# A decoder trunk on one core: the second layer's memory softmax turned by VectorE squares and transfers instead of TensorE transposes

## The chip, the core and the metric

The kernel runs on one core of a Trainium2 chip. A core has TensorE (PE, matrix products and transposes), VectorE (DVE), ScalarE (ACT), GpSimd (POOL) and SyncE (SP), which here issues DMA transfers. Each engine executes its own queue in order; engines wait for one another by semaphores. The metric is device microseconds of one execution.

## The reference

The reference is a trunk of two layers over 256 positions of width 2048, in float32. Layer A mixes with a gated spatial unit, layer B with latent attention (12 heads); beside either stands a cross-attention of 4 heads into 256 memory tokens, and after each a gated feed-forward part. The change concerns the memory heads of layer B, which stand beside the latent attention:

```python
def mla_attention(q_lat, g_q_lat, w_uq, w_uk, w_uv, c_kv, k_rope, cos, sin):
...
        qa = jnp.einsum('bqhn,rhn->bqhr', qn, w_uk)
        s = (jnp.einsum('bqhr,bkr->bhqk', qa, c_kv)
             + jnp.einsum('bqhp,bkp->bhqk', qr, k_rope)).astype(jnp.float32) * scale
        q_pos = i * Q_BLOCK + jnp.arange(Q_BLOCK)
        s = jnp.where(k_pos[None, :] <= q_pos[:, None], s, -jnp.inf)
        p = jax.nn.softmax(s, axis=-1).astype(c_kv.dtype)
        o_lat = jnp.einsum('bhqk,bkr->bqhr', p, c_kv)
        return jnp.einsum('bqhr,rhv->bqhv', o_lat, w_uv)
...

def memory_attention(q_m, mem, g_mem, w_mem_kv):
    B, S, _ = q_m.shape
    M = mem.shape[1]
    q = q_m.reshape(B, S, MEM_HEADS, MEM_HEAD_DIM)
    kv = rmsnorm(mem, g_mem) @ w_mem_kv
    k = kv[..., :MEM_W].reshape(B, M, MEM_HEADS, MEM_HEAD_DIM)
    v = kv[..., MEM_W:].reshape(B, M, MEM_HEADS, MEM_HEAD_DIM)
    s = jnp.einsum('bshd,bmhd->bhsm', q, k).astype(jnp.float32) * (MEM_HEAD_DIM ** -0.5)
    p = jax.nn.softmax(s, axis=-1).astype(v.dtype)
    return jnp.einsum('bhsm,bmhd->bshd', p, v).reshape(B, S, MEM_W)

...
        mo = memory_attention(q_m, mem, g_mem[l], w_mem_kv[l])
        x = x + jnp.concatenate([main, mo], axis=-1) @ w_out[l]
```

The memory's keys and values depend on no layer's activations and are made at the start.

## The kernel before

**Weights.** Nearly all the work is matrix products with weights that are streamed once from HBM. `chunk()` loads a piece of 512 KB (384 KB for `w_uq`) by a DMA on SP into a tile `raw`. ACT copies it, rounded, to `whi` (L124), and DVE makes the rest `wlo` = `raw` - `whi` (L125). There are four buffers each of `raw`, `whi` and `wlo`, so loads run a few pieces ahead of PE. PE multiplies both halves with activations that are split the same way (`mm_fm`, L161, L162 and L164; `gemm_tm`, L192 to L194). Right behind each load's issue `chunk()` calls `self.pending.some()`, which issues the transfers that were asked for behind that load, if any.

**The order.** The code is written stage by stage, and a scheduler lays each engine's instructions into one static order at compile time; the order of the code is a priority, not the final order. Where the code says `manual_schedule` for SP, SP's instructions stay in the order of the code.

**Layer B's loop.** The 12 latent heads go in six pairs. For pair i `queries(i)` loads two pieces of `w_uq` and makes the pair's queries; their rotary part is made by DVE (a shuffle L795, L797 to L799) and split by ACT and DVE (L868, L869). `keys(i)` loads a piece of `w_uk`. `scores(h)` makes a head's scores in PSUM (L887, L889); DVE adds the mask and takes the maximum (L894), ACT the exponential with its sum (L899), and DVE scales by the reciprocal of the sum (L902, L904). `turn(h)` transposes the probabilities in three blocks on PE (L911, against an identity) with a copy from PSUM by ACT (L913), and `attend(h)` multiplies with the values (L920, L921). In pair i the scores are those of pair i-1's heads, and the turns and products those of pair i-2's. `values()` loads two pieces of `w_uv`, in pairs 2 and 4.

**Memory heads of layer B.** One a pair, between that work: `memory_scores` (head i in pair i: scores L527, maximum L532, exponential L540, reciprocal L541, scaling by DVE L546), `memory_turn` in the next pair (four PE transposes of 128x128, L554, and a copy by ACT, L558), and `memory_out` one pair later (L565).

**Memory heads of layer A.** These are turned in another way. All four heads' probabilities lie in one tile `pm`, scaled by ACT (L544). DVE transposes each 32x32 block by itself with a stream transpose, 1024 columns at a time ("a square", L727), into a tile `small`; then sixteen transfers within SBUF (L731), 64 KB each in pieces of 128 bytes, set each block where the transposed matrix has it. They are issued on SP, two behind each of eight loads.

Of the kernel before, what the change touches and what calls it, by code (L numbers as in the profile page):

```python
# [8 lines left out]
F32 = mybir.dt.float32  # L9
# [62 lines left out]
class Pending(list):  # L72
# [4 lines left out]
    def ask(self, steps, counts):  # L77
        for n in counts:
            self.append(steps[:n])
            steps = steps[n:]  # L80
        assert not steps


class Kernel:
# [438 lines left out]
    def memory_scores(self, l, h, q, pool, p=None):  # L523
        nc = self.nc
        acc = self.psum()
        for sb in range(2):
            nc.tensor.matmul(  # L527
                acc[:, sb * S : (sb + 1) * S], q[:, sb * P : (sb + 1) * P], self.kT[l][:, h, :], start=True, stop=True
            )
        scale = 128 ** -0.5  # L530
        mx = self.tmp(pool, [P, 2], "mx", 4)
        nc.vector.tensor_reduce(mx, acc.rearrange("p (a m) -> p a m", a=2), AX.X, ALU.max)  # L532
        nc.vector.tensor_scalar(mx, mx, -scale, None, ALU.mult)
        by_act = p is not None
        if p is None:
            p = self.tmp(pool, [P, 2, 2, P], "mp", 2)
        a4 = acc.rearrange("p (a m c) -> p a m c", a=2, m=2)
        den = self.tmp(pool, [P, 2], "den", 4)
        for sb in range(2):
            nc.scalar.activation(p[:, sb], a4[:, sb], AF.Exp, bias=mx[:, sb : sb + 1], scale=scale, accum_out=den[:, sb : sb + 1])  # L540
        nc.vector.reciprocal(den, den)  # L541
        for sb in range(2):
            if by_act:
                nc.scalar.activation(p[:, sb], p[:, sb], AF.Copy, scale=den[:, sb : sb + 1])  # L544
            else:
                nc.vector.tensor_scalar(p[:, sb], p[:, sb], den[:, sb : sb + 1], None, ALU.mult)  # L546
        return p

    def memory_turn(self, p, pool, bufs=2):
        nc = self.nc  # L550
        acc = self.psum()
        for mb in range(2):
            for sb in range(2):
                nc.tensor.transpose(  # L554
                    acc[:, mb * S + sb * P : mb * S + (sb + 1) * P], p[:, sb, mb], self.ident
                )
        pT = self.tmp(pool, [P, 512], "pT", bufs)
        nc.scalar.activation(pT, acc, AF.Copy)  # L558
        return pT
# [102 lines left out]
    def layer_a(self):  # L662
# [4 lines left out]
        with ExitStack() as ctx:  # L667
# [50 lines left out]
            small = small.rearrange("p (b n c) -> p b n c", b=4, c=32)  # L718
            lanes = lambda i: slice(32 * i, 32 * i + 32)
# [5 lines left out]
            def squares(k):  # L725
                src = pm[:, 1024 * k : 1024 * (k + 1)].rearrange("p (n b c) -> p n b c", n=8, b=4)
                nc.vector.transpose(small[:, :, 8 * k : 8 * k + 8, :].rearrange("p b n c -> p n b c"), src)  # L727

            def place(q, b):
                out = pm[lanes(b)].rearrange("p (n q c) -> p n q c", n=16, q=4)[:, :, q, :]  # L730
                nc.sync.dma_start(out=out, in_=small[lanes(q), b])  # L731

# [4 lines left out]
            mhooks = {2: each(scores, 0, 1), 4: each(scores, 2, 3) + each(squares, 0)}, {0: each(squares, 1)}, {5: each(out, *range(MH))}  # L737
            for c in range(3):
# [11 lines left out]
                if c == 1:  # L750
                    self.pending.ask([lambda q=q, b=b: place(q, b) for q in range(4) for b in range(4)], [0] * 6 + [2] * 8)
# [5 lines left out]
    def layer_b(self):  # L757
# [9 lines left out]
        with tc.tile_pool(name="lb", bufs=1) as lb:  # L767
# [41 lines left out]
            acc = self.psum()[:, :S]  # L809
# [39 lines left out]
            qn, qr, kn, pa, pm = {}, {}, {}, {}, {}  # L849
# [73 lines left out]

            def mscores(h):
                pm[h] = self.memory_scores(1, h, qm[:, h, :], lp)

            def mturn(h):
                pm[h] = self.memory_turn(pm[h], lp, 3)

            def mout(h):  # L930
                self.memory_out(1, h, pm.pop(h), hl)

            n = GH // 2
            for i in range(n):
# [173 lines left out]
```

## Time and profile before

| what | value |
|---|---|
| median of three runs | 2045.46 us (2045.2 to 2045.59) |
| the profiled execution's own time | 2045.34 us |
| its span, first to last instruction | 2043.6 us |
| mean granted TensorE clock | 0.999 |
| busy: PE, DVE, ACT, POOL | 100%, 66%, 51%, 5% of the span |
| read from HBM | 387.88 MB, 191 GB/s over the span |
| layer B's pair loop (from the first memory head's scores to the last one's output) | 1145.39 to 1211.4 us |

A profile row names engine, source line, operation, the tile written and the tiles read, and a count. Times are microseconds from the span's start. A busy time of PE includes matmuls that wait inside its pipeline for one another, and a duration is longer than the distance between two starts, since the next instruction begins before the last has ended; so costs on a full engine are read from distances. An idle time before an instruction is given with the engine that ended it.

### The profile page before, as it was taken

To read this page: it belongs to the slowest core of one execution; us is meant where nothing else is said; L and a number is where in the kernel's file an instruction comes from. 1 tells how busy PE (TensorE), PEld (TensorE's weight loads), DVE (VectorE), ACT (ScalarE), POOL (GpSimd) and SP (SyncE) were. 2 spreads that over 40 slices of the span, in tenths; PEclk is the share of its full clock that TensorE was granted. 3 is DMA by queue.
4 is the path that set the end of the run, shared out by engine and by line. 5 is a ranking of instruction groups with operands and counts; after the bars stand their busy time and mean duration, and the time that the engine had idled before them with its cause. 6 is when DMAs were issued, how large, how long until landed. Compare 5 with 4: busy or idle time off the path is not lost.

```text
span 2043.6 us, 38986 instructions
## 1 busy us (share of the span) xinstructions
PE 2034.7 (100%) x16216; PEld 1968.7 (96%) x16216; DVE 1359.0 (66%) x1853; ACT 1042.7 (51%) x1347; POOL 94.5 (5%) x125
## 2 busy tenths in 40 slices
PE   9999999999999999999999999999999999999998
PEld 8989999999999999999999999999988999889997
DVE  6866667767656666457689875776655667656675
ACT  6754644555435454345545665455544455434553
POOL 0000013000000000000052001300000000000000
PEclk9999999999999999999999999999999999999999
DMA  8575855666666666566565544578766666566654
GB/s 309 188 228 175 196 181 186 204 190 194 197 193 190 197 195 196 191 195 194 188 196 182 174 130 155 186 206 219 225 196 195 188 200 191 194 196 188 197 185 155
DMA packets 228306, 395.67 MB, mean 194 GB/s; under 512 B 39328, under 2 KB 45856, under 8 KB 228000
## 3 DMA queue, kind: packets, MB, share of 16 engines
q1 hardware_dynamic: 227840, 392.65, 62.5%
q8 instruction: 127, 2.08, 0.4%
q14 instruction: 51, 0.42, 0.1%
q10 hardware_dynamic: 288, 0.52, 0.1%
HBM read 387.88 MB, written 2.10 MB: 191 GB/s over the span
## 4 chain that ended last, share of the span: by engine, by line
PE 99%; issue 0%; DVE 0%; ACT 0%; POOLq 0%; POOL 0%
PE ps L161 26%; PE ps L162 26%; PE ps L164 26%; PE ps L192 6%; PE ps L194 6%; PE ps L193 6%; PE ps L887 0%; PE ps L499 0%; PE ps L498 0%; PE ps L501 0%; PE ps L565 0%; PE ps L527 0%; PE ps L704 0%; PE ps L920 0%; PE ps L889 0%; PE ps L302 0%
## 5 line engine op out<-in xcount | busy, mean ns | idle before, releaser
L125 DVE TENSOR_TENSOR wlo<-raw,whi 128x1024 fp32r<-128x1024 f32 (+1 forms) x672 | 818.8, 1235 | 610.6 <-issue 408.8
L124 ACT ACTIVATE whi<-raw 128x1024 fp32r<-128x1024 f32 (+1 forms) x672 | 705.3, 1056 | 795.9 <-PE ps L162 583.7
L161 PE MATMUL ps<-xhl,whi 128*128 128x256 f32 x3264 | 752.1, 277 | 0.0
L162 PE MATMUL ps<-xhl,whi 128*128 128x256 f32 x3264 | 750.2, 276 | 0.0
L161 PEld LDWEIGHTS ps<-xhl,whi 128*128 128x128 f32 x3264 | 612.6, 188 | 0.3
L162 PEld LDWEIGHTS ps<-xhl,whi 128*128 128x128 f32 x3264 | 612.6, 188 | 0.3
L164 PE MATMUL ps<-xhl,wlo 128*128 128x256 f32 x3264 | 403.2, 276 | 0.0
L164 PEld LDWEIGHTS ps<-xhl,wlo 128*128 128x128 f32 x3264 | 385.1, 188 | 0.0
L161 PE MATMUL ps<-h,whi 128*128 128x256 f32 x704 | 161.6, 276 | 0.0
L162 PE MATMUL ps<-h,whi 128*128 128x256 f32 x704 | 161.5, 276 | 0.0
L620 DVE SCALAR_TENSOR_TENSOR c<-a,cT,c 128x255 f32<-128x255 f32 (+1 forms) x352 | 146.3, 479 | 0.0
L193 PE MATMUL ps<-wlo,h 128*128 128x512 f32 (+1 forms) x364 | 139.0, 382 | 0.0
L194 PE MATMUL ps<-whi,h 128*128 128x512 f32 (+1 forms) x364 | 138.7, 382 | 0.0
L192 PE MATMUL ps<-whi,h 128*128 128x512 f32 (+1 forms) x364 | 138.3, 382 | 0.0
L162 PEld LDWEIGHTS ps<-h,whi 128*128 128x128 f32 x704 | 131.9, 188 | 0.0
L161 PEld LDWEIGHTS ps<-h,whi 128*128 128x128 f32 x704 | 131.9, 188 | 0.0
L617 ACT ACTIVATE c<-a,cT 128x256 f32<-128x256 f32 x176 | 91.6, 591 | 77.1 <-DVE a L242 77.1
L161 PE MATMUL ps<-mainhl,whi 128*128 128x256 f32 x512 | 118.0, 277 | 0.0
L162 PE MATMUL ps<-mainhl,whi 128*128 128x256 f32 x512 | 117.9, 276 | 0.0
L162 PEld LDWEIGHTS ps<-mainhl,whi 128*128 128x128 f32 x512 | 96.1, 188 | 0.0
L161 PEld LDWEIGHTS ps<-mainhl,whi 128*128 128x128 f32 x512 | 96.1, 188 | 0.0
L164 PE MATMUL ps<-h,wlo 128*128 128x256 f32 x704 | 86.9, 276 | 0.0
(252 smaller groups left out, 1969.1 us busy)
## 6 DMA issues: line engine op xcount, KB each, us to landing
raw<-in_w_ffn_up SPq DMA_DIRECT2D x352, 512.0 KB, 4.1
raw<-in_w_ffn_down SPq DMA_DIRECT2D x176, 512.0 KB, 4.7
raw<-in_w_out SPq DMA_DIRECT2D x64, 512.0 KB, 4.4
raw<-in_w_in_a SPq DMA_DIRECT2D x56, 512.0 KB, 4.3
raw<-in_w_mem_kv SPq DMA_DIRECT2D x30, 512.0 KB, 5.4
raw<-in_w_in_b SPq DMA_DIRECT2D x16, 512.0 KB, 4.3
raw<-in_w_uq SPq DMA_DIRECT2D x12, 384.0 KB, 3.5
raw<-in_w_kv_a SPq DMA_DIRECT2D x8, 512.0 KB, 4.5
```

The costliest lines, as they stand in the source:

```text
L124: nc.scalar.activation(hi[:, :n], raw[:, :n], AF.Copy)
L125: nc.vector.tensor_tensor(lo[:, :n], raw[:, :n], hi[:, :n].bitcast(F32), ALU.subtract)
L161: mm(acc, wh, x[:, :S], start=first, stop=False)
L162: mm(acc, wh, x[:, S:], start=False, stop=False)
L164: mm(acc, wl, x[:, :S], start=False, stop=last)
L192: mm(acc, xh, wh, start=first, stop=False)
L193: mm(acc, xh, wl, start=False, stop=False)
L194: mm(acc, xl, wh, start=False, stop=last)
L617: nc.scalar.activation(c[:, i, :], a[:, i, :], AF.Identity, scale=w(2), bias=w(3))
L620: nc.vector.scalar_tensor_tensor(o, a[:, i, : S - 2 + j], w(j), o, ALU.mult, ALU.add)
```

## The change

Layer A's way of turning is made a class `Turn` (squares, transfers), and layer B uses it too. Layer A's work and its order stay as they were on every engine. In layer B:

- all four memory heads' scores are made in pair 0, into one stretch of the tile `scratch`, and scaled by ACT;
- the two squares are made in pair 1, into a new tile `small`;
- sixteen transfers within SBUF are asked for at pair 3, two behind each of the next eight loads; SP keeps the order of the code throughout the loop;
- the transposes and the copies of `memory_turn` are gone, and all four outputs are made behind the last pair.

```diff
+class Turn:
+    def __init__(self, nc, p, small, n):
+        self.nc, self.p, self.n = nc, p, n
+        self.small = small.rearrange("p (b n c) -> p b n c", b=4, c=32)
+
+    def squares(self, first, count):
+        src = self.p[:, first * P : (first + count) * P].rearrange("p (n b c) -> p n b c", n=count, b=4)
+        self.nc.vector.transpose(self.small[:, :, first : first + count, :].rearrange("p b n c -> p n b c"), src)
+
+    def place(self, q, b):
+        lanes = lambda i: slice(32 * i, 32 * i + 32)
+        out = self.p[lanes(b)].rearrange("p (n q c) -> p n q c", n=self.n, q=4)[:, :, q, :]
+        self.nc.sync.dma_start(out=out, in_=self.small[lanes(q), b])
+
+    def places(self):
+        return [lambda q=q, b=b: self.place(q, b) for q in range(4) for b in range(4)]
 
 
 class Kernel:
...
-    def memory_scores(self, l, h, q, pool, p=None):
+    def memory_scores(self, l, h, q, pool, p):
...
-        by_act = p is not None
-        if p is None:
-            p = self.tmp(pool, [P, 2, 2, P], "mp", 2)
         a4 = acc.rearrange("p (a m c) -> p a m c", a=2, m=2)
         den = self.tmp(pool, [P, 2], "den", 4)
         for sb in range(2):
             nc.scalar.activation(p[:, sb], a4[:, sb], AF.Exp, bias=mx[:, sb : sb + 1], scale=scale, accum_out=den[:, sb : sb + 1])
         nc.vector.reciprocal(den, den)
         for sb in range(2):
-            if by_act:
-                nc.scalar.activation(p[:, sb], p[:, sb], AF.Copy, scale=den[:, sb : sb + 1])
-            else:
-                nc.vector.tensor_scalar(p[:, sb], p[:, sb], den[:, sb : sb + 1], None, ALU.mult)
-        return p
-
-    def memory_turn(self, p, pool, bufs=2):
-        nc = self.nc
-        acc = self.psum()
-        for mb in range(2):
-            for sb in range(2):
-                nc.tensor.transpose(
-                    acc[:, mb * S + sb * P : mb * S + (sb + 1) * P], p[:, sb, mb], self.ident
-                )
-        pT = self.tmp(pool, [P, 512], "pT", bufs)
-        nc.scalar.activation(pT, acc, AF.Copy)
-        return pT
+            nc.scalar.activation(p[:, sb], p[:, sb], AF.Copy, scale=den[:, sb : sb + 1])
...
+            pm = scratch[:, 2 * GW : 2 * GW + MH * 512]
+            memory = Turn(nc, pm, lp.tile([P, MH * 512], F32, name="small"), 4 * MH)
+
             def mscores(h):
-                pm[h] = self.memory_scores(1, h, qm[:, h, :], lp)
-
-            def mturn(h):
-                pm[h] = self.memory_turn(pm[h], lp, 3)
+                self.memory_scores(1, h, qm[:, h, :], lp, pm[:, 512 * h : 512 * (h + 1)].rearrange("p (m a c) -> p a m c", m=2, a=2))
 
             def mout(h):
-                self.memory_out(1, h, pm.pop(h), hl)
-
-            n = GH // 2
-            for i in range(n):
-                queries(i)
-                keys(i)
-                if i >= 2:
-                    turn(2 * i - 4)
-                    turn(2 * i - 3)
-                if i in (2, 4):
-                    values(i // 2)
-                if i >= 1:
-                    scores(2 * i - 2)
-                    scores(2 * i - 1)
-                if i >= 2:
-                    attend(2 * i - 4)
-                    attend(2 * i - 3)
-                if i < MH:
-                    mscores(i)
-                if 1 <= i <= MH:
-                    mturn(i - 1)
-                if 2 <= i <= MH + 1:
-                    mout(i - 2)
+                self.memory_out(1, h, pm[:, 512 * h : 512 * (h + 1)], hl)
+
             each = lambda f, *hs: [lambda h=h: f(h) for h in hs]
-            for f in each(scores, 10, 11) + each(turn, 8, 9):
-                f()
-            hooks = {0: each(attend, 8, 9) + each(turn, 10, 11), 2: each(attend, 10, 11)}
-            self.w_out(1, hl, [12, 13, 14, 15] + list(range(12)), hooks)
+            run = lambda fs: [f() for f in fs]
+            with tc.manual_schedule(engines={mybir.EngineType.SP}):
+                for i in range(GH // 2):
+                    if i == 3:
+                        self.pending.ask(memory.places(), [2] * 8)
+                    queries(i)
+                    keys(i)
+                    if i == 0:
+                        run(each(mscores, *range(MH)))
+                    if i == 1:
+                        run([lambda k=k: memory.squares(8 * k, 8) for k in range(2)])
+                    if i >= 2:
+                        run(each(turn, 2 * i - 4, 2 * i - 3))
+                    if i in (2, 4):
+                        values(i // 2)
+                    if i >= 1:
+                        run(each(scores, 2 * i - 2, 2 * i - 1))
+                    if i >= 2:
+                        run(each(attend, 2 * i - 4, 2 * i - 3))
+                run(each(mout, *range(MH)) + each(scores, 10, 11) + each(turn, 8, 9))
+                hooks = {0: each(attend, 8, 9) + each(turn, 10, 11), 2: each(attend, 10, 11)}
+                self.w_out(1, hl, [12, 13, 14, 15] + list(range(12)), hooks)
             ctx.close()
 
     def run(self):
```

The first place is SP's queue around the fourth pair's loads of `w_uq` (`raw` is the tile that a load fills; the line numbers of the changed program differ). Before, from the last piece of `w_uv`:

```order
L114 DMA raw_13827<-in_w_uv 128x2x512
L114 DMA raw_13920<-in_w_uq 128x2x384
L114 DMA raw_13944<-in_w_uq 128x2x384
L114 DMA raw_13983<-in_w_uk 128x4x256
L114 DMA raw_14099<-in_w_uq 128x2x384
```

Changed; the transfers are the rows with `scratch<-small`:

```order
L132 DMA raw_13847<-in_w_uv 128x2x512
L132 DMA raw_13915<-in_w_uq 128x2x384
L96 DMA scratch<-small 32x16x32 x2
L132 DMA raw_13941<-in_w_uq 128x2x384
L96 DMA scratch<-small 32x16x32 x2
L132 DMA raw_13982<-in_w_uk 128x4x256
L96 DMA scratch<-small 32x16x32 x2
L132 DMA raw_14075<-in_w_uq 128x2x384
```

The pair's second load of `w_uq` now stands behind the first two transfers, and each of the following loads behind two more. The transfers read what both squares have written.

The second place is DVE in pair 0, from the first memory head's maximum; before, one maximum stood there between two `wlo` and the other heads' came a pair apart. Changed:

```order
L550 TENSOR_REDUCE mx_13540<-ps_13537 128x2
L550 TENSOR_REDUCE mx_13552<-ps_13549 128x2
L551 TENSOR_SCALAR mx_13540<-mx_13540 128x2
L550 TENSOR_REDUCE mx_13564<-ps_13561 128x2
L551 TENSOR_SCALAR mx_13552<-mx_13552 128x2
L551 TENSOR_SCALAR mx_13564<-mx_13564 128x2
L556 RECIPROCAL den_13543<-den_13543 128x2
L556 RECIPROCAL den_13555<-den_13555 128x2
L143 TENSOR_TENSOR wlo_13613<-raw_13611,whi_13612 128x768
L556 RECIPROCAL den_13567<-den_13567 128x2
L785 STREAM_SHUFFLE rs_13493<-ps_13442 128x256
L787 TENSOR_TENSOR rm_13495<-ps_13442,cosT 128x256
```

Three heads' maxima, and then three reciprocals that wait for ACT's exponentials, now stand together. On ACT the table load, the three heads' six exponentials and the first head's two scalings stand ahead of the next `whi` of 1024 columns, which came ahead of the table load before.

The third place is DVE ahead of PE's first `turn`, where the probabilities of latent heads 0 and 1 (`p_13652` and `p_13670` before, `p_13692` and `p_13710` now) are scaled. Before:

```order
L894 ISA p_13670,mx_13668<-ps_13661,mask 128x256
L894 ISA mx_13668 128x1
L532 TENSOR_REDUCE mx_13682<-ps_13679 128x2
L897 TENSOR_SCALAR mx_13668<-mx_13668 128x2
L902 RECIPROCAL den_13651<-den_13651 128x2
L533 TENSOR_SCALAR mx_13682<-mx_13682 128x2
L904 TENSOR_SCALAR p_13652<-p_13652,den_13651 128x128
L904 TENSOR_SCALAR p_13652<-p_13652,den_13651 128x256
L125 TENSOR_TENSOR wlo_13829<-raw_13827,whi_13828 128x1024
L902 RECIPROCAL den_13669<-den_13669 128x2
```

Changed:

```order
L143 TENSOR_TENSOR wlo_13849<-raw_13847,whi_13848 128x1024
L887 TENSOR_SCALAR mx_13708<-mx_13708 128x2
L785 STREAM_SHUFFLE rs_13771<-ps_13720 128x256
L787 TENSOR_TENSOR rm_13773<-ps_13720,cosT 128x256
L892 RECIPROCAL den_13691<-den_13691 128x2
L143 TENSOR_TENSOR wlo_13917<-raw_13915,whi_13916 128x768
L788 TENSOR_TENSOR rs_13771<-rs_13771,sinT 128x256
L894 TENSOR_SCALAR p_13692<-p_13692,den_13691 128x128
L894 TENSOR_SCALAR p_13692<-p_13692,den_13691 128x256
L892 RECIPROCAL den_13709<-den_13709 128x2
L789 TENSOR_TENSOR rm_13773<-rm_13773,rs_13771 128x256
L143 TENSOR_TENSOR wlo_13943<-raw_13941,whi_13942 128x768
```

The two pieces end and begin differently because the same scaling stands later in the queue: the `wlo` of the second piece of `w_uv` (1024 columns), which followed head 0's scaling, is now ahead of it, with the shuffle and two products of pair 2's rotary part and the `wlo` of the fourth pair's first piece of `w_uq` (768 columns). Head 1's scaling now comes behind the `wlo` of that pair's second piece. Both squares lie ahead of this too, the first behind the fourth head's maximum, the second between the masked maxima of heads 0 and 1. On PE the scores of memory heads 0 to 2 stand together in pair 0 and head 3's behind pair 1's queries; the four outputs stand together behind the loop; the rest keeps its order but for the place of a few blocks.

More of the change, by code (lines that the diff above doesn't have):

```diff
@@ L717, in layer_a @@
             pm, small = (la.tile([P, MH * 512], F32, name=name) for name in ("pm", "small"))
-            small = small.rearrange("p (b n c) -> p b n c", b=4, c=32)
-            lanes = lambda i: slice(32 * i, 32 * i + 32)
+            turned = Turn(nc, pm, small, 4 * MH)
             def scores(h):
@@ L723, in scores @@
                 self.memory_scores(0, h, qm[:, h, :], la, view)
[L725 to L731, printed above, removed]
             def out(h):
@@ L736, in layer_a @@
             each = lambda f, *hs: [lambda h=h: f(h) for h in hs]
-            mhooks = {2: each(scores, 0, 1), 4: each(scores, 2, 3) + each(squares, 0)}, {0: each(squares, 1)}, {5: each(out, *range(MH))}
+            mhooks = {2: each(scores, 0, 1), 4: each(scores, 2, 3) + [lambda: turned.squares(0, 8)]}, {0: [lambda: turned.squares(8, 8)]}, {5: each(out, *range(MH))}
             for c in range(3):
@@ L750, in layer_a @@
                 if c == 1:
-                    self.pending.ask([lambda q=q, b=b: place(q, b) for q in range(4) for b in range(4)], [0] * 6 + [2] * 8)
+                    self.pending.ask(turned.places(), [0] * 6 + [2] * 8)
                 with tc.manual_schedule(engines={mybir.EngineType.SP}) if c else nullcontext():
@@ L848, in layer_b @@
             scale = HD ** -0.5
-            qn, qr, kn, pa, pm = {}, {}, {}, {}, {}
+            qn, qr, kn, pa = {}, {}, {}, {}
             def queries(pr):
```

## The prediction

> **What bounds the kernel now.** I read the page first, then a table of windows around the loop that changes, then the chain of waits there, then the engines' timelines row by row.
>
> ```profile
> span 2043.6 us, 38986 instructions
> PE 2034.7 (100%) x16216; PEld 1968.7 (96%) x16216; DVE 1359.0 (66%) x1853; ACT 1042.7 (51%) x1347; POOL 94.5 (5%) x125
> PE 99%; issue 0%; DVE 0%; ACT 0%; POOLq 0%; POOL 0%
> 1160.00:1170.00 10.00, 10.00 (x79) 9.68 (x78) 9.50 (x33) 7.86 (x22) 0.00 (x0) 1.00 0.41 111
> 1170.00:1180.00 10.00, 10.00 (x57) 8.76 (x56) 5.79 (x20) 6.29 (x17) 0.00 (x0) 1.00 0.60 170
> ```
>
> TensorE (PE) is busy for the whole span and is 99% of the chain that ended last. So only two things can move the time: work taken off PE, and a wait put on it. The two window rows (columns: stretch, length, PE, PEld, DVE, ACT, POOL busy, clock, DMA share, GB/s) show the stretch of the pair loop that matters. PE is full in both, but VectorE (DVE), whose mean over the span is 66%, is busy for 9.50 of 10 us just before 1170. DVE has almost no room there, and it executes its queue in order. Everything below follows from these two facts.
>
> **What is removed.** The four memory heads' transposes leave PE. In the chain of waits (start, us, what) they are:
>
> ```profile
> 1158.29 0.86 PE ps L527 x4
> 1159.15 0.44 PE ps L554 x4
> 1179.11 0.44 PE ps L554 x4
> 1192.28 0.44 PE ps L554 x4
> 1210.08 0.44 PE ps L554 x4
> ```
>
> Four times 0.44 is **1.76 us**, and PE has no other removal: the score matmuls (L527, 0.86 a head) and the output matmuls are moved, not removed. The copies of the transposed blocks that leave ACT, the scaling that goes from DVE to ACT and the changed place of the output matmuls touch engines with idle time or keep PE's amount the same; I cost them at nothing on PE except through the DVE queue, which comes next. So 1.76 us, 0.09% of the time, is the most that this change can gain.
>
> **What is added ahead of the first turn.** The first thing after the moved work for which PE waits on DVE is the turn of heads 0 and 1: their probabilities must have been scaled. In the timelines before (start, us, engine, line, what, idle before):
>
> ```profile
> 1163.78 0.55 DVE L904 TENSOR_SCALAR p<-p,den 128x128 f32<-128x128 f32 x2
> 1164.31 1.22 DVE L125 TENSOR_TENSOR wlo<-raw,whi 128x1024 fp32r<-128x1024 f32 x1
> 1165.46 0.16 DVE L902 RECIPROCAL den<-den 128x2 f32<-128x2 f32 x1
> 1166.38 0.54 DVE L904 TENSOR_SCALAR p<-p,den 128x128 f32<-128x128 f32 x2
> 1168.39 0.60 PE L911 MATMUL ps<-ident,p 128*128 128x128 f32 x4
> ```
>
> DVE scaled head 0 by 1164.33 and head 1 by 1166.92; PE took head 0 at 1168.39. The cover was 4.06 us for head 0. PE comes there later in the changed kernel: all four heads' scores lie ahead, where two did, and one transpose group less: 1168.39 + 2 x 0.86 - 0.44 = **1169.67**. Head 1's first block is then wanted three transposes later, 0.33 us by the 0.44 of four, at 1170.0.
>
> Now DVE. Its durations, as distances from one start to the next where it did not idle, and ACT's:
>
> ```profile
> 1146.35 0.69 DVE L532 TENSOR_REDUCE mx<-ps 128x2 f32<-128x512 f32 x1
> 1149.45 1.23 DVE L125 TENSOR_TENSOR wlo<-raw,whi 128x1024 fp32r<-128x1024 f32 x1 [0.78 <-ACT whi L124]
> 1151.79 0.17 DVE L541 RECIPROCAL den<-den 128x2 f32<-128x2 f32 x1 [1.11 <-ACT mp L540]
> 1152.88 0.41 DVE L797 TENSOR_TENSOR rm<-ps,cosT 128x256 f32<-128x256 f32 x1
> 1153.20 0.95 DVE L125 TENSOR_TENSOR wlo<-raw,whi 128x768 fp32r<-128x768 f32 x1
> 1154.07 0.42 DVE L798 TENSOR_TENSOR rs<-rs,sinT 128x256 f32<-128x256 f32 x1
> 1157.86 0.87 DVE L869 TENSOR_TENSOR qr<-rm,qr 64x256 fp32r<-64x256 f32 x2
> 1161.46 0.29 DVE L894 CUSTOM_DVE_ANT_0 p<-ps,mask 128x128 f32<-128x128 f32 x1 [0.25 <-PE ps L889]
> 1162.14 0.17 DVE L897 TENSOR_SCALAR mx<-mx 128x2 f32<-128x2 f32 x1
> 217.13 1.24 DVE L727 STREAM_TRANSPOSE small<-pm 128x1024 f32<-128x1024 f32 x1
> 1148.36 1.06 ACT L124 ACTIVATE whi<-raw 128x1024 fp32r<-128x1024 f32 x1 [0.48 <-PE ps L162]
> 1149.44 1.28 ACT L540 ACT_TABLE_LOAD   x1
> 1150.73 0.47 ACT L540 ACTIVATE mp<-ps,mx 128x256 f32<-128x256 f32 x1
> 215.16 1.71 ACT L544 ACTIVATE pm<-pm,den 128x256 f32<-128x256 f32 x4
> ```
>
> From these: a wlo of 1024 columns 1.15 (1164.31 to 1165.46), of 768 columns 0.87 (1153.20 to 1154.07), a rotary step of 256 columns 0.33, a subtraction pair for qr 0.87, a head's masked maximum 0.68 (1161.46 to 1162.14), a memory head's maximum about 0.6, a square about 1.2, a scaled head 0.55, the two-column operations about 0.09. On ACT an exponential is 0.47 and a scaling 0.43 (1.71 for four).
>
> First ACT holds DVE up. Before, ACT made whi at 1148.36 and then took one head's two exponentials. Now the order puts the table load, six exponentials and head 0's two scalings ahead of that whi. The maximum of head 0 is there at about 1147.8 (1146.35, the second maximum behind it, 2 x 0.6, and the small ones), so whi ends at 1147.8 + 1.28 + 6 x 0.47 + 2 x 0.43 + 1.06 = 1153.8, where DVE's wlo of it began at 1149.45 before. DVE has only the other two maxima, a wlo and three rotary steps to fill that time and idles for over 3 us, against 0.78 and 1.11 there before.
>
> From 1153.8 the DVE queue up to head 0's scaled probabilities holds, by the changed order: four wlo of 1024 (4.6), three of 768 (2.6), two squares (2.4), one memory maximum (0.6), two masked maxima (1.4), eight rotary steps (2.65), two pairs for qr (1.75), small ones (0.45) and the scaling itself (0.55): 17.0 us, so head 0 is ready at 1170.8, and with 0.3 for short waits at **1171.1**. The squares are 2.4 of this; as much again is a wlo of 1024, one of 768 and three rotary steps (3.0) which the scheduler has pulled ahead of the scaling. PE, there at 1169.67, waits about **1.4 us**.
>
> **The second wait runs through SP.** Head 1's scaling stands behind another wlo of 768 columns, that of the fourth pair's second load. In the changed order this load stands on SP's queue behind the first two of the sixteen transfers, and these wait for the second square. By the list above that square ends 11.6 us behind 1153.8, at about 1165.6 with short waits. What a transfer and a load behind it take, from layer A, where the same sixteen run now (DMA views around 219.5 us, then the pair loop's loads, then all five first loads among layer A's transfers):
>
> ```profile
> 218.39 1.42 SPq L731 DMA_DIRECT2D pm<-small  x2
> 1155.38 2.51 SPq L114 DMA_DIRECT2D raw<-in_w_uq  x2
> raw<-in_w_in_a SPq DMA_DIRECT2D x1, 512.0 KB, 4.9
> DMA to landing us min/median/max: 3.2/3.6/4.7
> DMA to landing us min/median/max: 4.9/6.9/7.8
> ```
>
> Two transfers keep SP for 1.4 us, so the load, issued by 1157.9 before, is issued at about 1167. It lands 3.2 us later at the least (the fastest of the loop's loads), 4.9 us if it fares like the first load behind two transfers: 1170.2 to 1171.9. Then whi (0.85, by the 768 of 1024 columns), wlo and scaling, 0.87 + 0.55: 1172.5 to 1174.2. DVE alone does not allow it before 1171.1 + 0.09 + 0.33 + 0.87 + 0.55 = 1172.9. I take **1173.7**, the nearer to the slower landing, since that row is the same situation. PE's two waits together are then 1173.7 - 1170.0 = **3.7 us** (1.4 at head 0 and 2.3 at head 1), between 2.9 and 4.2 by the bounds.
>
> [...]
>
> Behind the turn there is cover again: the value matmuls follow it, DVE is busy for 5.79 of 10 us in the next window, and the later loads, even at the 7.8 us of layer A, are wanted a pair later. The transfers' results are read only after the last pair.
>
> **The clock.** Two waits with 0.33 us of work between them leave PE almost idle for 4 us. What that does is shown only at the two ends of the span:
>
> ```profile
> 1.11 4.63 PE L302 MATMUL ps<-ones 128*128 128x128 f32 x20 [1.11 <-DVE ones L293]
> 6.70 0.39 PE L162 MATMUL ps<-memhl,whi 128*128 128x256 f32 x1
> 6.91 0.30 PE L161 MATMUL ps<-memhl,whi 128*128 128x256 f32 x1
> 7.04 0.28 PE L162 MATMUL ps<-memhl,whi 128*128 128x256 f32 x1
> 2035.00:2036.00 1.00, 0.78 (x7) 0.57 (x5) 0.93 (x4) 0.00 (x0) 0.00 (x0) 1.00 0.31 127
> 2037.00:2038.00 1.00, 0.00 (x0) 0.00 (x0) 0.34 (x1) 0.34 (x1) 0.56 (x1) 0.93 0.98 401
> ```
>
> PE's last work ends at 2035.78, and by the mean of 0.93 the granted clock began to fall at about 2037.9, 2.1 us later. At the start the same matmul came every 0.21 us up to 6.91 and every 0.13 from there, so a slow clock costs half of PE's time while it lasts, and it can last the 5.8 us from PE's first work at 1.11. A fall here would thus cost between nothing (if it recovers at once) and 2.9 us; I take the middle, 1.4. One idle of 1.4 us would be too short by these rows; 3.7 us of 4.0 is not.
>
> [...]
>
> **The sum**, from the profiled execution's own 2045.34 us (the runs' median is 2045.46, so the two agree within 0.1): 2045.34 - 1.76 + 3.7 + 1.4 = **2048.7 us**. Its own range is 2046.5 to 2050.7: the waits at 2.9 to 4.2, the clock at 0 to 2.9.
>
> **The rivals.**
>
> The clock holds. The waits come as said and PE keeps its rate: 2045.34 - 1.76 + 3.7 = 2047.3 us. For it: each wait by itself is shorter than the 2.1 us after the last matmul or as long. Against it: together they are nearly twice that.
>
> DVE catches up. Its idle time before the turn takes the squares and the maxima, nothing arrives late, and the gain stays: 2045.34 - 1.76 = 2043.6 us. For it: 4.06 us of cover, and idle of 0.78, 1.11 and 0.25 in the rows. Against it: 9.50 of 10 us busy, and 3.0 us of other work pulled ahead of the scaling on top of the squares. This would be the best outcome, and still not a measurable one.
>
> The load is later still, and the kernel slower. The fourth pair's second load shares the DMA engines with the transfers and lands as the slowest of layer A's, after 7.8 us: 1167 + 7.8 + 0.85 + 0.87 + 0.55 = 1177.1, PE waits 7.1 us, the clock certainly falls: 2045.34 - 1.76 + 7.1 + 1.4 = 2052.1 us. It decides, with the 1.4, from a landing of about 5.1 us on (waits above 4.57 make the kernel slower by 0.2%). Against it: in layer A only loads behind further transfers took so long, and this one is behind the first two.
>
> **How the numbers follow.** Chances: the forecast 0.48, the clock holding 0.31, DVE catching up 0.08, the late load 0.13. A change under 0.2%, 4.1 us, can hardly be told from none in this kernel, so slower begins at 2049.55 and faster ends at 2041.4. Faster would need more than twice all that PE loses: 0.01. Slower takes the late load and the upper quarter of the forecast (a fallen clock that costs over 2.3 us): 0.13 + 0.13 = 0.26. The rest, 0.73, is no change. The range leaves out the case without waits at the bottom and the worst of the late load at the top: 2045.4 to 2051.2.
>
> **What would show it.** Right: idle time of PE in front of the transposes of the heads' probabilities, first about 1.4 us, then about 2.3 us, released by DVE's scaling; DVE's scaling of head 0 some 7 us later than before; the fourth pair's second load issued nearly 10 us later; PE elsewhere without a wait; the matmuls behind the second wait at 0.21 to 0.23 us instead of 0.11 to 0.12 if the clock falls. Wrong: no idle of PE there (then DVE idled less than I say), an idle in front of the output matmuls (then the transfers are late), or a time below 2043.

## The result, and the profile after

| | before | changed |
|---|---|---|
| median of 20 runs | 2045.30 us (2044.87 to 2045.85) | 2049.03 us (2046.94 to 2050.82) |
| ratio | | 1.0018, 95% interval 1.0011 to 1.0025 |
| profiled execution, span | 2045.34, 2043.6 us | 2049.83, 2048.1 us |
| mean granted clock of the profiled execution | 0.999 | 0.997 |

The changed kernel is 3.7 us slower at the median, a little under 0.2%. Its runs also scatter four times as wide as those of before: 18 of 20 lie between 2048.3 and 2050.8 us with a mean clock of 0.997 or 0.998, and the two fastest, 2046.94 and 2047.24 us, are the only ones with 0.999.

PE's waits in the profile after (what PE waited for, by whom it was released, us in total, times, longest):

```profile
PE ps L901 <- ACT qr L858: 2.6, 1, 2.6
PE ps L901 <- DVE p L894: 1.2, 1, 1.2
PE ps L320 <- DVE ones L311: 1.1, 1, 1.1
```

The last is the program's start, and was there before. The two new ones stand in front of the first turn (L901 is L911 of before), and nowhere else does PE wait. PE's timeline there:

```profile
1168.24 1.07 PE L182 MATMUL ps<-chl,wlo 128*128 128x256 f32 x8
1170.47 0.70 PE L901 MATMUL ps<-ident,p 128*128 128x128 f32 x3 [1.16 <-DVE p L894]
1173.72 0.45 PE L901 MATMUL ps<-ident,p 128*128 128x128 f32 x1 [2.56 <-ACT qr L858]
1173.82 0.77 PE L210 MATMUL ps<-whi,chl 128*128 128x512 f32 x1
1174.39 0.63 PE L211 MATMUL ps<-wlo,chl 128*128 128x512 f32 x1
1179.09 0.43 PE L210 MATMUL ps<-whi,chl 128*128 128x512 f32 x1
1179.35 0.40 PE L211 MATMUL ps<-wlo,chl 128*128 128x512 f32 x1
1179.59 0.40 PE L212 MATMUL ps<-whi,chl 128*128 128x512 f32 x1
```

PE waits 1.16 us for head 0, does three transposes, and waits 2.56 us for head 1. Then the value matmuls, which came every 0.23 us before, come every 0.43 us up to 1179.1 and every 0.23 again from there. The twelve matmuls from 1173.82 to 1179.09 take 5.27 us; behind a turn without a wait, in the run with the scores moved only (below), twelve take 2.85, so 2.4 us are lost. The windows of the same execution show the granted clock in that stretch (the third number from the end):

```profile
1172.00:1173.00 1.00, 0.00 (x0) 0.00 (x0) 0.58 (x1) 1.00 (x3) 0.00 (x0) 0.66 0.87 285
1178.00:1179.00 1.00, 1.00 (x4) 0.80 (x3) 0.00 (x0) 0.00 (x0) 0.00 (x0) 0.50 1.08 229
1179.00:1180.00 1.00, 1.00 (x5) 0.78 (x4) 0.00 (x0) 0.63 (x1) 0.00 (x0) 0.93 1.17 237
```

The clock is 0.50 in every window between, from 1173 to 1179, and 1.00 from 1166 to 1172 and from 1180 to 1184. So the mean of 0.66 puts the fall at 1172.32, 0.93 the return at 1179.14.

On DVE, the rows that set the two waits:

```profile
1153.68 1.23 DVE L143 TENSOR_TENSOR wlo<-raw,whi 128x1024 fp32r<-128x1024 f32 x1 [0.48 <-ACT whi L142]
1164.07 1.24 DVE L91 STREAM_TRANSPOSE small<-scratch 128x1024 f32<-128x1024 f32 x1
1170.13 0.55 DVE L894 TENSOR_SCALAR p<-p,den 128x128 f32<-128x128 f32 x2
1172.42 0.96 DVE L143 TENSOR_TENSOR wlo<-raw,whi 128x768 fp32r<-128x768 f32 x1 [1.35 <-ACT whi L142]
1173.30 0.54 DVE L894 TENSOR_SCALAR p<-p,den 128x128 f32<-128x128 f32 x2
```

Head 0 is scaled 6.35 us later than before (1170.13 against 1163.78), head 1 6.9 us later. Between them DVE idles 1.35 us for one whi. Where that whi comes from, the chain of waits tells (start, us, what):

```profile
1164.15 1.17 DVE small L91
1165.39 0.60 SPq L96
1166.04 1.11 SPq L96
1167.20 4.25 DMA raw<-in_w_uq
1171.54 0.84 ACT whi L142
```

The second square, two transfers issued by SP, the load of `w_uq` behind them, its whi. The profile names ACT's qr as what ended the 2.56 us, since that was the last to end before PE went on (1173.62); the block that PE transposes there is DVE's p, whose first part was scaled from 1173.30, and in the first two experiments the same wait carries DVE's name. PE's start follows that of head 1's scaling by 0.42 to 0.43 us here and in both of them (1173.30 to 1173.72, 1172.49 to 1172.92, 1171.50 to 1171.92).

The sum of the profiled execution: 2045.34 - 1.76 for the transposes + 3.72 for the waits + 2.4 for the clock = 2049.7, measured 2049.83. That it closes so well is partly luck: within the loop alone the same terms fall 0.6 us short (end of the experiments), and the two executions differ by half a microsecond outside it.

### The profile page after: what moved, and what is told of

It is laid out like the page before. It is cut to its first block, busy times and chain, and to the rows that moved or that the text cites. A ratio compares the mean times of both kernels' runs of the same rounds, so it can differ in the third digit from the quotient of the medians.

```text
span 2048.1 us, 38967 instructions
## 1 busy us (share of the span) xinstructions
PE 2035.3 (99%) x16200; PEld 1967.7 (96%) x16200; DVE 1359.4 (66%) x1847; ACT 1042.5 (51%) x1351; POOL 94.5 (5%) x125
## 4 chain that ended last, share of the span: by engine, by line
PE 98%; DMA 1%; DVE 1%; ACT 0%; issue 0%; SPq 0%; POOLq 0%; POOL 0%; ACTq 0%
PE ps L179 26%; PE ps L180 26%; PE ps L182 26%; PE ps L210 6%; PE ps L211 6%; PE ps L212 6%; DMA raw<-in_w_mem_kv 0%; PE ps L877 0%; PE ps L564 0%; PE ps L517 0%; PE ps L516 0%; PE ps L519 0%; PE ps L545 0%; PE ps L703 0%; PE ps L910 0%
```

## The experiments

Two theories were set against each other. The queue theory: the waits come from the order of DVE's queue, and the loss of clock from the waits. The transfer theory: the sixteen transfers themselves cost the time, by loading the DMA engines. Times are medians of 6 to 11 executions, with the kernel before on the same chip at 2045.21 (first four) or 2045.32 us (the others).

**Transfers later.** The transfers start two loads later, behind the third load instead of the first, so the fourth pair's second load no longer stands behind them.

```diff
-                        self.pending.ask(memory.places(), [2] * 8)
+                        self.pending.ask(memory.places(), [0] * 2 + [2] * 8)
```

> The sixteen transfers are asked for two loads later, so the fourth pair's second load of w_uq no longer stands behind any of them on SP; DVE's queue is unchanged. If the second wait runs through SP and that load (queue theory): the load is issued by about 1159.5 as before, the wlo in front of head 1's scaling finds its data, and head 1 is scaled about 1.4 us earlier, at 1170.6 + 0.1 + 0.3 + 0.9 + 0.5 = 1172.4. First wait 1.2 us unchanged, second about 1.1 instead of 2.6: 2045.3 - 1.76 + 2.3 = 2045.8 us while the clock holds, up to 2047.5 in executions in which it falls. If the transfers as such cost the time, by loading the DMA engines (transfer theory): they still run in this stretch, so the waits stay and the time stays near 2049.

Measured: 2046.29 us (2045.92 to 2048.1), ratio 1.0007 (0.9998 to 1.0017). PE's waits and DVE's rows of the profiled execution:

```profile
PE ps L901 <- DVE p L894: 2.3, 2, 1.2
1171.62 0.95 DVE L143 TENSOR_TENSOR wlo<-raw,whi 128x768 fp32r<-128x768 f32 x1
1172.49 0.54 DVE L894 TENSOR_SCALAR p<-p,den 128x128 f32<-128x128 f32 x2
```

The wlo no longer idles for its whi, the second wait is 1.11 us instead of 2.56, the first is unchanged at 1.17. All sixteen transfers still run. Six executions lie at 2045.9 to 2046.4 with a clock of 0.999, four at 2047.4 to 2048.1 with 0.998: with less idle time the clock falls in some executions only. The load was issued at about 1162.4, not at 1159.5 as expected, which was still early enough, and two of these four lie above the 2047.5 that was expected as the most.

**Four behind four.** The transfers are bunched.

```diff
-                        self.pending.ask(memory.places(), [2] * 8)
+                        self.pending.ask(memory.places(), [4] * 4)
```

> Four transfers behind each of four loads instead of two behind each of eight. SP stands longer on the transfers and the fourth pair's second load is issued about 1.3 us later still. In the order that results, DVE's wlo of that load has moved behind head 1's scaling; nothing else on DVE moves. Queue theory: the order decides and not the load, so head 1 is scaled right behind head 0, at 1170.6 + 0.1 + 0.3 + 0.5 = 1171.5; waits 1.2 and 0.7, 2045.3 - 1.76 + 1.9 = 2045.4 us with the clock at full rate. Transfer theory: a later load and denser transfers make it slower, 2049.0 + 1.3 = 2050.3 us.

Measured: 2045.39 us (2044.95 to 2045.57), ratio 1.0001 (0.9992 to 1.0010). PE waited 1.16 and 0.24 us, and DVE's rows show why:

```profile
PE ps L901 <- DVE p L894: 1.4, 2, 1.2
1171.50 0.54 DVE L894 TENSOR_SCALAR p<-p,den 128x128 f32<-128x128 f32 x2
1173.88 0.96 DVE L143 TENSOR_TENSOR wlo<-raw,whi 128x768 fp32r<-128x768 f32 x1 [1.84 <-ACT whi L142]
```

The four transfers keep SP for 2.61 us where two kept it for 1.76, so the load is issued at 1168.57, later than in the changed kernel (1167.20). The wlo idles longer for it, 1.84 us, but it now stands behind head 1's scaling, where PE does not wait. The transfer theory, which asked for 2050.3, falls here: denser transfers and a later load made the kernel 3.6 us faster than the changed one. The mean clock was 0.999 in all ten executions, which spread over 0.6 us.

**Filled waits.** The changed kernel with useless transposes of the identity on PE, overwritten at once.

```diff
                 acc = self.psum()
+                for _ in range({0: 10, 1: 21}.get(h, 0)):
+                    nc.tensor.transpose(acc[:, :P], self.ident, self.ident)
                 for i in range(3):
```

> The changed kernel with 31 further transposes of the identity on PE around the first turn, 10 for head 0 and 21 for head 1, whose results are overwritten; 31 x 0.11 = 3.4 us of work that nothing needs. Clock theory (the granted clock falls because PE idles): the useful work still comes at 1170.5 and 1173.8, but the clock stays at full rate, so 2045.3 - 1.76 + 3.7 = 2047.2 us in all executions, with little spread: added work makes the kernel 1.8 us faster than the median of 2049.0. Rival (the value matmuls behind the wait are slow because the transfers compete for the memory): they stay at 0.43 us each and the time stays at 2049.0, or 2049.0 + 3.4 if PE isn't idle there at all.

Measured: 2046.73 us (2046.35 to 2047.15), ratio 1.0008 (0.9998 to 1.0017). PE's timeline:

```profile
1169.62 2.67 PE L901 MATMUL ps<-ident 128*128 128x128 f32 x23
1172.57 0.93 PE L901 MATMUL ps<-ident 128*128 128x128 f32 x7
1173.25 0.48 PE L210 MATMUL ps<-whi,chl 128*128 128x512 f32 x1
1173.57 0.39 PE L211 MATMUL ps<-wlo,chl 128*128 128x512 f32 x1
1173.80 0.39 PE L212 MATMUL ps<-whi,chl 128*128 128x512 f32 x1
1173.00:1174.00 1.00, 1.00 (x8) 0.90 (x7) 0.97 (x4) 0.86 (x2) 0.00 (x0) 1.00 1.31 258
```

The scheduler mixed the blocks: head 0's transposes come only at 1172.13, and head 1's at 1174.50, among the value matmuls. But the useless transposes fill the stretch in which PE idled, the granted clock is 1.00 there (last row) and over the whole stretch from 1169 to 1178, and the value matmuls come every 0.23 us, beside the same transfers as in the changed kernel (mean DMA share from 1173 to 1178 1.17 here, 1.16 there). So their 0.43 us was the clock and not the memory. Added work made the kernel 2.3 us faster than the changed one, and the spread is down to 0.8 us.

**Heads apart.** Heads 0, 1 and 2, and 3 in the first three pairs, the squares behind them, the transfers behind the last pair's loads.

```diff
-                    if i == 3:
-                        self.pending.ask(memory.places(), [2] * 8)
+                    if i == 5:
+                        self.pending.ask(memory.places(), [6, 6, 4])
...
-                    if i == 0:
-                        run(each(mscores, *range(MH)))
-                    if i == 1:
-                        run([lambda k=k: memory.squares(8 * k, 8) for k in range(2)])
...
                         run(each(attend, 2 * i - 4, 2 * i - 3))
+                    run(each(mscores, *{0: [0], 1: [1, 2], 2: [3]}.get(i, [])))
+                    if i in (1, 2):
+                        memory.squares(8 * i - 8, 8)
```

> The same way of turning, spread out: memory head 0's scores in pair 0, heads 1 and 2 in pair 1, head 3 in pair 2; the first square in pair 1, the second behind head 3; all sixteen transfers behind the last pair's three loads (6, 6 and 4). In the resulting order one square and two maxima are gone from DVE's queue ahead of the first turn, and no load that is wanted soon stands behind a transfer. Queue theory: no wait of PE, the clock holds and the whole 1.76 us are gained: 2043.5 us. Transfer theory: six transfers at a time on a queue of loads leave some wait, 2045 us or more.

> The version with the heads spread over three pairs, timed in more rounds to tell its difference from the kernel before from none: queue theory 2043.5 us or a little less (2043.27 in its first ten executions), with all executions below the fastest of before (2044.8) and a ratio of 0.9991.

Measured: 2043.27 us (2042.97 to 2043.67), ratio 0.9991 (0.9981 to 1.0), and on another chip 2043.31 us (2043.12 to 2043.83), ratio 0.9991 (0.9982 to 1.0). This beats both kernels: the slowest of its 21 executions is a microsecond faster than the fastest of the 54 of before beside them (2044.82). It is still only 0.1%. DVE, PE and SP there:

```profile
1164.27 0.55 DVE L894 TENSOR_SCALAR p<-p,den 128x128 f32<-128x128 f32 x2
1164.96 0.55 DVE L894 TENSOR_SCALAR p<-p,den 128x128 f32<-128x128 f32 x2
1168.99 1.24 DVE L91 STREAM_TRANSPOSE small<-scratch 128x1024 f32<-128x1024 f32 x1
1168.71 0.82 PE L901 MATMUL ps<-ident,p 128*128 128x128 f32 x6
1187.05 3.95 SPq L96 DMA_DIRECT2D scratch<-small  x6
```

Both heads are scaled 3.9 and 3.2 us before PE takes them at 1168.71, both squares stand behind their scaling (the expectation had one of them ahead), and six transfers in a row keep SP for 3.95 us without a load behind them making PE wait. PE waits for nothing in the loop.

**Scores moved only.** All four heads' scores in the first pair, scaled by ACT, but turned by PE as before.

```diff
-                    if i == 3:
-                        self.pending.ask(memory.places(), [2] * 8)
-                    if i == 1:
-                        run([lambda k=k: memory.squares(8 * k, 8) for k in range(2)])
...
+            def mturn(h):
+                p = pm[:, 512 * h : 512 * (h + 1)]
+                acc = self.psum()
+                for k in range(4):
+                    nc.tensor.transpose(acc[:, k * P : (k + 1) * P], p[:, k * P : (k + 1) * P], self.ident)
+                nc.scalar.activation(p, acc, AF.Copy)
...
+                    if 1 <= i <= MH:
+                        mturn(i - 1)
```

> One part of the change alone: all four memory heads' scores in the first pair and scaled by ACT, outputs behind the loop, but turned by PE transposes and a copy by ACT, one head a pair, as before; no squares, no transfers. It tells which part of the longer DVE queue makes the first wait. If it takes the squares (2.4 us of DVE): head 0 is scaled about 2.5 us before PE comes to it, only head 1 can be late by some 0.4 us, and without the gain of 1.76 us the time is 2045.3 to 2045.8 us. If the three heads' exponentials on ACT and the maxima alone are enough: a first wait of 1 us or more stays, 2046.3 us or more.

Measured: 2045.08 us (2044.88 to 2045.24), ratio 0.9998 (0.9989 to 1.0008). No wait:

```profile
1163.59 0.28 DVE L884 CUSTOM_DVE_ANT_0 p<-ps,mask 128x128 f32<-128x128 f32 x1
1167.29 0.55 DVE L894 TENSOR_SCALAR p<-p,den 128x128 f32<-128x128 f32 x2
1169.70 0.54 DVE L894 TENSOR_SCALAR p<-p,den 128x128 f32<-128x128 f32 x2
1168.83 1.07 PE L182 MATMUL ps<-chl,wlo 128*128 128x256 f32 x8
1169.74 0.68 PE L901 MATMUL ps<-ident,p 128*128 128x128 f32 x4
1170.18 0.48 PE L210 MATMUL ps<-whi,chl 128*128 128x512 f32 x1
```

Head 0 is ready 1.9 us before PE comes (2.5 were expected), and the time is 0.2 us below the expected stretch. The moved scores eat more than half of the 4.06 us of cover that there was, and cost nothing. In the changed kernel the scaling stands 2.84 us later, and head 0's masked maximum, further ahead in the queue, tells where that comes from:

```profile
1163.51 0.28 DVE L884 CUSTOM_DVE_ANT_0 p<-ps,mask 128x128 f32<-128x128 f32 x1
```

Up to that maximum the two runs are level (1163.59 and 1163.51), although the changed kernel has done its first square by then (1155.76 to 1156.92): the first square cost no time up to there. That it filled time in which DVE otherwise idles was not shown. The whole delay arises behind it. There stand the second square, 1.16 us to the next start (1164.07 to 1165.23), and one wlo of 768 columns with three rotary steps, 1.86 us by the prediction's prices, which the changed kernel's order has ahead of head 0's scaling and this run's has behind it. So what makes the first wait is one square and the work that was pulled ahead; no run has the one without the other.

**Scaled by VectorE.** One part undone: DVE scales the memory probabilities again.

```diff
         for sb in range(2):
-            nc.scalar.activation(p[:, sb], p[:, sb], AF.Copy, scale=den[:, sb : sb + 1])
+            if l == 0:
+                nc.scalar.activation(p[:, sb], p[:, sb], AF.Copy, scale=den[:, sb : sb + 1])
+            else:
+                nc.vector.tensor_scalar(p[:, sb], p[:, sb], den[:, sb : sb + 1], None, ALU.mult)
```

> The changed kernel with layer B's memory probabilities scaled by DVE again (eight operations of 256 columns, 2.4 us, more on DVE; as much less on ACT). Queue theory: 2.4 us more in the queue ahead of head 0's scaling, and in the order that results both wlo of the fourth pair, the second of them fed by the load behind two transfers, stand ahead of it. So one long wait of about 5.5 us at head 0 in place of 1.2 and 2.6, almost none at head 1, and the clock falls in every execution: 2045.3 - 1.76 + 5.7 = 2049.2, plus 1 to 2.9 for the clock, 2050 to 2052 us. If the scaling's place did not matter (DVE has 34% idle on average): 2049.0 us.

Measured: 2051.38 us (2050.53 to 2051.92), ratio 1.0029 (1.0018 to 1.0041). One wait, and the wlo that idles for the load behind two transfers is ahead of head 0 too:

```profile
PE ps L904 <- DVE p L897: 5.3, 1, 5.3
1173.06 0.96 DVE L143 TENSOR_TENSOR wlo<-raw,whi 128x768 fp32r<-128x768 f32 x1 [1.86 <-ACT whi L142]
1174.62 0.55 DVE L897 TENSOR_SCALAR p<-p,den 128x128 f32<-128x128 f32 x2
```

So the scaling by ACT, which is part of the change, is worth about 2.3 us in it, with the order that it brings.

**All of them in one sum.** From the first memory score to the first product of `w_out` the loop took, in the profiled executions, by such pairs of rows (here before's and the changed kernel's):

```profile
1145.23 1.02 PE L527 MATMUL ps<-kT,qm 128*128 128x256 f32 x4
1225.69 0.36 PE L161 MATMUL ps<-mainhl,whi 128*128 128x256 f32 x1
```

```profile
1144.98 1.24 PE L545 MATMUL ps<-kT,qm 128*128 128x256 f32 x5
1230.42 0.37 PE L179 MATMUL ps<-mainhl,whi 128*128 128x256 f32 x1
```

| kernel | loop, us | against before | transposes | waits | clock |
|---|---|---|---|---|---|
| before | 80.46 | | | | |
| changed | 85.44 | +4.98 | -1.76 | 3.72 | 2.4 |
| transfers later (clock fell) | 83.06 | +2.60 | -1.76 | 2.28 | 1.7 |
| four behind four | 80.65 | +0.19 | -1.76 | 1.40 | 0 |
| scaled by VectorE | 87.30 | +6.84 | -1.76 | 5.30 | 3.0 |
| scores moved only | 80.52 | +0.06 | 0 | 0 | 0 |
| heads apart | 78.62 | -1.84 | -1.76 | 0 | 0 |

The clock's share is an estimate, half of the time from the last wait's end to the clock's return, since a value matmul took 0.43 us at a clock of 0.50 and 0.23 at 1.00, but for the changed kernel, where it is from the matmul rows. The terms give the measured difference to 0.1 us without a wait, and fall 0.3 to 0.6 us short of it with one.

The rest lies in how a wait is read. An idle time starts where the last duration ends, and PE's durations are longer than the distance to the next start (0.40 us against 0.24 for the value matmul at 1179.35, 0.63 against 0.43 for the one at 1174.39), so an idle time is less than what the wait costs. Distances leave nothing out. In the run with the scores moved only, where PE does not wait, it is 1.35 us from the start of the eight matmuls ahead of the turn (1168.83) to the first value matmul (1170.18), with four transposes between, and 2.85 us on to the thirteenth. In the changed kernel the first distance is 5.58 us (1168.24 to 1173.82), 4.23 more, and the second 5.27, 2.42 more. Read in this way:

| kernel | waits | value matmuls | with -1.76 | measured |
|---|---|---|---|---|
| changed | 4.23 | 2.42 | +4.89 | +4.98 |
| transfers later | 2.78 | 1.56 | +2.58 | +2.60 |
| four behind four | 1.88 | 0 | +0.12 | +0.19 |
| scaled by VectorE | 6.07 | 2.34 | +6.65 | +6.84 |

With the filled waits the loop took 82.01 us, 1.55 more than before; -1.76 and 3.4 for the 31 useless transposes make 1.64.

## Why the prediction was right

The time was 2049.03 us, 0.3 above the forecast of 2048.7, and by the mechanism that was forecast. The mechanism is shown; that the sizes of the terms add up so closely is in part luck, as said at the terms.

- **The gain of 1.76 us.** Shown by the version without waits: -1.94 and -2.01 us at the medians, -1.84 in the loop. The prediction called 1.76 the most that the change can gain; the 0.1 to 0.2 us above it are not explained.
- **ACT holds up the wlo of 1024 columns.** Forecast 1153.8, measured 1153.68. DVE idled for 2.7 us there, where over 3 were forecast.
- **The first wait.** Head 0 ready at 1171.1, measured 1170.7 (1170.13 + 0.55); wait 1.4, measured 1.16. Two errors hide in that: PE was done with the work ahead at 1169.31, not 1169.67, and it began at 1170.47, behind the first of the scaling's two parts, where the prediction had it wait for both. The cause lies in DVE's queue, as the run without squares shows. The prediction had named both parts of it, the squares and the work pulled ahead; of the squares, only the second delays the turn.
- **The second wait.** Square ended at 1165.6, measured 1165.3; load issued at 1167, measured 1167.20; landing within 3.2 to 4.9 us, measured 4.25 (the 4.9 were those of a load of 512 KB, and this one has 384); wait 2.3, measured 2.56. That it runs through SP and this load is shown by the run with the transfers later, and that it does so only because the wlo stands ahead of the scaling by four behind four.
- **The two waits together.** 3.7, measured 3.72 as idle time. The agreement is luck: the small errors of the two cancelled, and the forecast was not an idle time but a delay, from 1170.0, where PE would want head 1, to 1173.7. PE took head 1 at 1173.72, but it would have been there half a microsecond earlier than forecast, so the delay was 4.23 us by the distances, at the top of the range of 2.9 to 4.2.
- **The clock.** Taken at 1.4, between 0 and 2.9. In the profiled execution it was 2.4. At the median it was about 1.3 (2049.03 - 2045.30 + 1.76 - 4.23), or 1.8 with the idle time of 3.72 in place of 4.23, if the waits of all executions were those of the profiled one; in two of twenty executions it was nothing. The 1.4 was the middle between two bounds, and that the median came out near it is luck: how long the clock stays down differs from execution to execution (its mean was 0.997 in eight of the 18 in which it fell, 2049.56 to 2050.82 us, and 0.998 in ten, 2048.34 to 2049.14 us). That the fall is the cause of the slow matmuls is shown by the filled waits, 0.23 us each at a clock of 1.00. The slow rate itself was taken from the start of the span, where the windows show a granted clock of 1.00, so it was inferred there from distances alone, and no run shows the clock as their cause; in the changed kernel the same matmuls of the start came every 0.11 to 0.12 us from 5.62 on. Behind the waits of the changed kernel rate and clock go together, 0.43 us at a clock of 0.50 and 0.23 at 1.00.
- **The rivals.** The clock holding was put at 2047.3; the two executions in which it held gave 2046.94 and 2047.24. DVE catching up did not happen. The late load did not either: 4.25 us, where it had to pass 5.1 (5.3 by the prediction's own terms, 1170.0 + 4.57 - 0.55 - 0.87 - 0.85 - 1167). The sentence that one idle of 1.4 us would be too short for the clock fits four behind four, 1.16 and 0.24 us, in which it never fell.

In the profiled execution the clock stayed down for 6.82 us (1172.32 to 1179.14). The row of the kernel's end, by which 3.7 us of waits in 4.0 would be enough, was a fair guide: with waits of 1.16 and 2.56 us and three transposes between them the clock fell, as it did in 18 of 20 executions.

## What to carry to other kernels

On a kernel whose matrix engine is full, work moved off it to an engine that is "66% busy" can be paid for where that engine is full: here 1.76 us less work on PE brought 4.23 us of waits and 2.42 us of slow matmuls. What counted was the busy time of the 10 us in front of the next place where the matrix engine waits for it (9.50 us of DVE before the change), and what stands ahead of the awaited instruction in its queue, above all an instruction that itself waits for a load (the wlo that idled 1.35 us ahead of head 1's scaling). A transfer put on the load queue made the loads behind it wait for what it waited for (SP stood 6.1 us for the second square), and in these runs that reached the matrix engine only through an instruction that stood in such a place. And waits of 2.3 to 5.3 us cost 1.6 to 2.4 us more through the clock in the profiled executions in which it fell, so a change that saves little must add no wait at all; here the same idea spread over three pairs kept its whole gain.

## What the runs showed of the hardware

Two short waits made the granted clock fall. By the mean clock it fell in 4 of 10 executions of the kernel whose profile has waits of 1.17 and 1.11 us with three transposes between them, in 18 of 20 with 1.16 and 2.56, in 6 of 6 with one of 5.3, and in none of 10 with 1.16 and 0.24. From the end of the work ahead of the turn it was 3.0 us to the fall in the changed kernel (1169.31 to 1172.32) and in the one with the transfers later (1169.93 to 1172.96), with three transposes in between, 0.70 us, and 4.5 us without work in the one scaled by VectorE (1169.66 to 1174.20). With four behind four PE took head 1 2.1 us behind that end (1169.82 to 1171.92), with the same three transposes in between, and the clock did not fall. The same kernel does not always do it, as the 4 of 10 show.

In the three profiled falls the clock went to 0.50 and came back to 1.00. In the run with the transfers later and in the one scaled by VectorE (windows; the third number from the end is the clock, here and below one kernel each):

```profile
1172.00:1173.00 1.00, 0.08 (x2) 0.12 (x2) 1.00 (x3) 0.95 (x3) 0.00 (x0) 0.98 0.94 116
1176.00:1177.00 1.00, 1.00 (x5) 0.78 (x5) 0.00 (x0) 0.00 (x0) 0.00 (x0) 0.81 1.13 313
```

```profile
1174.00:1175.00 1.00, 0.04 (x1) 0.04 (x1) 0.91 (x5) 1.00 (x5) 0.00 (x0) 0.60 1.28 206
1181.00:1182.00 1.00, 1.00 (x6) 0.83 (x5) 0.00 (x0) 0.60 (x1) 0.00 (x0) 0.98 1.14 260
```

By the means of the clock it was down from 1172.96 to 1176.38, 3.42 us, and from 1174.20 to 1181.04, 6.84 us; in the changed kernel it was 6.82. In these three the fall came ahead of the last wait's end, or 0.04 us behind it with the transfers later (1172.92 and 1172.96), and the slow value matmuls cost 1.6 to 2.4 us on top of the waits. With useless work in the gap (the filled waits) the mean clock was 0.999 in all ten executions.

Where the order of an engine is made by a scheduler, a small edit elsewhere can move it: with four transfers behind each load in place of two, head 1's scaling came ahead of the wlo of the late load, and the second wait went from 2.56 to 0.24 us. ACT's order moved too, by one copy (kn) ahead of that load's whi. Whether the changed kernel with the swap on DVE alone and its own transfers would do as well was not tried, since the order followed from the program and was not set by hand.
